# Taking the tensor work off GpSimd, and moving the adaLN gate from the output weights to the output

## The chip, the cores and the metric

One Trainium2 chip, one of its cores. The time of a kernel is the device time of one execution in microseconds (us), as the median of several runs. The engines are TensorE (PE, with its weight loads as PEld), VectorE (DVE), ScalarE (ACT), GpSimd (POOL) and SyncE (SP), which issues all DMAs here.

## The reference

One decoder layer on 256 tokens of width 1024, all in float32. The attention parts are left out here; there are two groups of 8 heads with 64 columns each, and group A has a mixture of dilated causal windows, group B plain causal attention (at 256 tokens there is only one block).

```python
mod = c @ w_ada + b_ada                          # (1, 3072)
shift, scale, gate = jnp.split(mod, 3, axis=-1)
h = x * (1.0 + scale) + shift
qa, ka, va, ga, qb, kb, vb, gb = jnp.split(h @ w_in, offs, axis=-1)   # 8 x 512 columns
qa, ka, qb, kb = _rope(qa), _rope(ka), _rope(qb), _rope(kb)
o_a = dilated_mixture(qa, ka, va) * silu(ga)
o_b = moba_attention(qb, kb, vb) * silu(gb)
y = jnp.concatenate([o_a, o_b], -1) @ w_out
x = layernorm(ALPHA * x + gate * y, ln_g, ln_b)
```

## The kernel before

**Precision.** A float32 matrix product is made of three products of a faster format (float32r). Each weight tile of 128 x 1024 (a buffer `raw`, 512 KB) is split: ACT copies it rounded to a buffer `whi`, and DVE or POOL subtracts that from the tile to get `wlo`, mostly in halves of 512 columns. `hH` and `hL` are the same two parts of h, `ogh` and `ogl` those of the gated attention output. PE multiplies `whi` with both parts of the other operand and `wlo` with its high part. `split_tile` is the function that splits; the lists `sp`, `wopool` in CFG say which subtractions POOL makes: 25 of 512 columns.

**Stages.** The first 60 us make h and its product with 1792 columns of w_in (q, k, v of group A and half of A's gate) in seven PSUM banks, `acc1`. Then come nine sets of 256 columns (list SETS), eight k-tiles each, and between their products PE gets the steps of eight attention pairs (two heads each): `att_pair` transposes the rotated q and k on PE (line 572 of before), `att_scores` multiplies them, DVE adds the mask and finds the maximum (`z`, line 598), ACT makes the exponentials (line 601), DVE a reciprocal (line 606), ACT scales; `att_trans` transposes the result (line 621), `att_pv` multiplies with v, DVE applies the silu gate (`og`) and the difference `ogl`. The rope is two DVE instructions: a product out of PSUM with a table (`pp`, line 514), which also frees the PSUM bank, and a sum of its halves (`rot`, line 256). `out_mm` multiplies with the eight row tiles of w_out, and `layer_norm(0)` and `layer_norm(1)` finish the token halves t=0 and t=1. Their parts are cut by CUTS: two of 512 columns for t=0; 512, 256, 256 for t=1.

**The gate.** `gate_acc(r)` adds c times one row tile of the last third of w_ada to a 128 x 1024 tile `gate`: ten halves by one DVE instruction each, six by a scaling on ACT and an addition on POOL. `gate_bcast` sums it over the partitions, by four products with a tile of ones (`onesr`), and `split_wo` multiplies each row tile of w_out by the result before it is split: seven halves and two whole tiles on DVE, five halves on POOL. ACT multiplies x by ALPHA (`scale_x`), and the layer norm adds that to y out of PSUM.

**What sets the order.** Nothing is decided at run time. The class `Plan` takes the operations in program order with a cost in ns for each (the first number given to `op`, `mm` or `tt`), works out due times from those of PE, and places one operation after another on its engine, with buffers from small pools: eight `raw`, six `whi`, six `wlo`, eight PSUM banks (`ps`), four `rot`. Each engine then executes its list in that order and waits by semaphores, so an instruction that waits holds up everything behind it on its engine. SP issues loads in the order of the `load_...` calls, each as soon as its `raw` buffer is free, and waits there otherwise. Lines 251 and 253 are copies on ACT, 256 two-operand operations on DVE or POOL (`tt`), 277 matmuls, 317 the loads.

Of the kernel before, what the change touches and what calls it, by code (L numbers as in the profile page):

```python
# [24 lines left out]
CFG = dict(raw=8, hdve=[3, 5, 6, 7], hl=6, a0=-6.0, ra=0.885, rb=1.15, s0=1, s1=5, gpos=1, wpool=[],  # L25
           sp=[[1, 2], [1, 2], [0, 1], [0, 1, 3], [1, 2], [0, 1], [1, 2], [0, 1, 3], [0, 1]],
           ropea=[0, 0, 0, 0], wopool=[[1], [0], [0], [1], [], [], [0], [1]], nf=2,
           jpe=[0, 1, 2, 0, 1, 1, 0, 2], pvo=[1, 0], pe0=1280, lock=1, wact=[], wsub=[], sact=[2, 6],
           ssub=[17], oact=[], osub=[0], gwhole=[1, 3], hamc=3300, lat=140, nst=4, nprob=2, nrot=4, nz=3,
           mact=[1, 2, 4, 5, 6], gdve=[1, 2, 3, 4, 6], nact=[0, 1, 2, 3], ropeb=[0, 1, 1, 1], norm='dve',  # L30
           t0=19000, late=0, lnp=1, warm=28, pt=2, wgpool=[[0], [0], [1], [0], [0], [], [0], [0]])
# [12 lines left out]
class Plan:  # L44
# [44 lines left out]
    def emit(self):  # L89
# [52 lines left out]
        def place(i):  # L142
# [37 lines left out]
            order.append((i, now, fin))  # L180

# [38 lines left out]
def hybrid_kernel(ctx: ExitStack, tc: tile.TileContext, x, c, w_in, w_out, w_ada, b_ada, ln_g, ln_b,  # L220
# [67 lines left out]
    onesr = consts.tile([128, 128], F32R)  # L288
# [81 lines left out]
    def modulate(k):  # L370
# [96 lines left out]
    def split_set(i, u):  # L467
# [3 lines left out]
                   2 * i + u in CFG["ssub"], [q for q in range(2) if 2 * u + q in CFG["sp"][i]])  # L471

    def split_wo(r):
        hi, lo = T["woh", r] = hi_lo()
        b = T["wo", r]
        for qs, cs in [((0, 1), slice(0, 1024))] if r in CFG["gwhole"] else [((q,), slice(q * 512, q * 512 + 512)) for q in range(2)]:
            e = POOL if len(qs) == 1 and qs[0] in CFG["wgpool"][r] else DVE
            tt(e, lambda cs=cs: b.ap[:, cs], lambda cs=cs: b.ap[:, cs], lambda cs=cs: gate[:, cs], OP.mult,
               vcost(e, cs.stop - cs.start), [("gate", q) for q in qs] + [(b, 0)], [(b, 0)])
        split_tile(hi, lo, b, lambda: b.ap, 1024, r in CFG["oact"], r in CFG["osub"], CFG["wopool"][r])  # L480

    def gate_acc(r):
        b = T["gate", r]
        for n in range(2):
            cs = slice(n * 512, (n + 1) * 512)
            if r in CFG["gdve"]:
                op(DVE, 663, lambda cs=cs: nc.vector.scalar_tensor_tensor(
                    gate[:, cs], b.ap[:, cs], cc[:, r:r + 1], gate[:, cs], op0=OP.mult, op1=OP.add),
                    [(b, n), "c", ("gate", n)], [("gate", n)], p2=True)
                continue  # L490
            copy(lambda cs=cs: b.ap[:, cs], lambda cs=cs: b.ap[:, cs], 613, [(b, n), "c"], [(b, n)],
                 scale=lambda: cc[:, r:r + 1])
            tt(POOL, lambda cs=cs: gate[:, cs], lambda cs=cs: gate[:, cs], lambda cs=cs: b.ap[:, cs], OP.add,
               1225, [(b, n), ("gate", n)], [("gate", n)])
# [14 lines left out]
    def rope_group(key, srcs, eng):  # L509
# [359 lines left out]
```

## Time and profile before

| what | value |
|---|---|
| median of 3 runs | 186.26 us (186.22 to 186.55) |
| profiled execution | 186.19 us |
| its span, first to last instruction | 184.3 us |
| mean granted TensorE clock | 0.951 |
| busy: PE / DVE / ACT / POOL | 164.2 / 144.2 / 107.5 / 67.2 us |

The span is what the views of the trace divide up; 1.89 us of the profiled execution lie around it. A busy time is the union of an engine's instructions. The granted clock is given as a share of TensorE's full speed: 1.00 is its upper level of 2.4 GHz, and about 0.5 its lower one of 1.2 GHz.

### The profile page before, as it was taken

What the parts mean: (1) busy time and instruction counts of PE and PEld (TensorE: products, weight loads), DVE (VectorE), ACT (ScalarE), POOL (GpSimd) and SP (SyncE); (2) the same over time, 40 slices, a digit from 0 to 9 for tenths busy, and PEclk for the clock granted to TensorE, in tenths of its full rate; (3) what the DMA queues carried; (4) which work ended last, traced back from release to release, by engine and by line L of the source; (5) the groups of instructions that cost most, each with busy time, mean ns of one, the idle gap of its engine ahead of it and who ended that gap; (6) DMA issues with size and microseconds to landing.
All of it is one profiled execution on the core that took longest, in us unless ns stands there. A gap on an engine that the chain in (4) does not pass through costs nothing.

```text
span 184.3 us, 3133 instructions
## 1 busy us (share of the span) xinstructions
PE 164.2 (89%) x1061; PEld 137.9 (75%) x1061; DVE 144.2 (78%) x305; ACT 107.5 (58%) x263; POOL 67.2 (36%) x55
## 2 busy tenths in 40 slices
PE   7758898899999999939999999999999859999950
PEld 2346786688888899927989689789988648778840
DVE  1449789899998699999489994569797983487883
ACT  3044744556666965715897689995489463990000
POOL 3000000000000897580033685970359980041460
PEclk9999999999999999975999999999999965999995
DMA  3999999999999999266457777670600600000022
GB/s 98 267 327 358 322 331 345 340 327 325 341 350 349 348 348 378 74 225 185 136 183 234 237 244 268 218 241 8 211 17 5 228 0 0 0 4 0 0 114 114
DMA packets 33429, 37.31 MB, mean 202 GB/s; under 512 B 1645, under 2 KB 28293, under 8 KB 33414
## 3 DMA queue, kind: packets, MB, share of 16 engines
q1 hardware_dynamic: 33414, 37.12, 63.3%
q8 instruction: 8, 0.13, 0.3%
q14 instruction: 7, 0.06, 0.1%
HBM read 36.07 MB, written 1.05 MB: 201 GB/s over the span
## 4 chain that ended last, share of the span: by engine, by line
PE 59%; DVE 14%; DMA 14%; SPq 5%; ACT 2%; POOL 2%; issue 2%; DVEq 0%; ACTq 0%
PE ps L277 54%; DMA raw<-in_w_in_dram 10%; DVE wlo L256 6%; SPq L317 5%; DMA raw<-in_w_ada_dram 4%; PE ps L621 3%; DVE rot L256 3%; POOL wlo L256 2%; PE ps L572 2%; DVE pp L514 1%; ACT whi L251 1%; DVE ogl L256 1%; DVE z L598 0%; DVE raw L693 0%; DVE raw L696 0%
## 5 line engine op out<-in xcount | busy, mean ns | idle before, releaser
L256 POOL TENSOR_TENSOR wlo<-raw,whi 128x512 fp32r<-128x512 f32 x25 | 37.9, 1542 | 86.4 <-DVE hL L256 58.3
L251 ACT ACTIVATE whi<-raw 128x512 fp32r<-128x512 f32 (+1 forms) x82 | 45.5, 612 | 17.0 <-DMA raw<-in_w_in_dram 12.0
L256 DVE TENSOR_TENSOR wlo<-raw,whi 128x512 fp32r<-128x512 f32 (+2 forms) x57 | 47.8, 866 | 8.0 <-ACT whi L251 7.8
L277 PE MATMUL ps<-whi,hH 128*128 128x256 f32 (+1 forms) x144 | 40.2, 335 | 2.1 <-ACT hH L251 1.9
L277 PE MATMUL ps<-wlo,hH 128*128 128x256 f32 (+1 forms) x144 | 41.9, 337 | 0.0
L277 PE MATMUL ps<-whi,hL 128*128 128x256 f32 (+1 forms) x144 | 40.0, 329 | 0.0
L277 PEld LDWEIGHTS ps<-whi,hH 128*128 128x128 f32 x144 | 26.6, 196 | 5.6 <-ACT hH L251 3.0
L277 PEld LDWEIGHTS ps<-whi,hL 128*128 128x128 f32 x144 | 26.6, 194 | 3.2 <-issue 1.4
L277 PEld LDWEIGHTS ps<-wlo,hH 128*128 128x128 f32 x144 | 26.7, 196 | 2.6 <-issue 1.4
L383 DVE SCALAR_TENSOR_TENSOR acc<-raw,cc,acc 128x256 f32<-128x256 f32 x49 | 23.6, 483 | 3.0 <-ACT acc L253 1.7
L601 ACT ACTIVATE prob<-z,st 128x256 f32<-128x256 f32 (+1 forms) x32 | 14.2, 447 | 11.8 <-DVE st L598 6.3
L277 PE MATMUL ps<-hL,whi 128*128 128x256 f32 x64 | 17.8, 300 | 0.0
L277 PE MATMUL ps<-hH,whi 128*128 128x256 f32 x64 | 17.5, 292 | 0.0
L277 PE MATMUL ps<-hH,wlo 128*128 128x256 f32 x64 | 17.0, 291 | 0.0
L253 ACT ACTIVATE prob<-prob,st 128x256 f32<-128x256 f32 (+1 forms) x32 | 12.1, 444 | 3.4 <-DVE st L606 3.3
L277 PE MATMUL ps<-whi,ogh 128*128 128x512 f32 (+1 forms) x40 | 12.9, 362 | 0.0
L277 PE MATMUL ps<-wlo,ogh 128*128 128x512 f32 (+1 forms) x40 | 12.8, 365 | 0.0
L277 PEld LDWEIGHTS ps<-hH,whi 128*128 128x128 f32 x64 | 11.7, 190 | 1.5 <-issue 1.2
L598 DVE CUSTOM_DVE_ANT_0 z<-ps,mask_t 128x256 f32<-128x256 f32 (+1 forms) x32 | 9.6, 348 | 3.7 <-PE ps L277 3.7
L277 PEld LDWEIGHTS ps<-hL,whi 128*128 128x128 f32 x64 | 11.6, 190 | 1.2 <-issue 1.0
L277 PE MATMUL ps<-whi,ogl 128*128 128x512 f32 (+1 forms) x40 | 12.4, 356 | 0.0
L277 PEld LDWEIGHTS ps<-hH,wlo 128*128 128x128 f32 x64 | 11.7, 191 | 0.3
(84 smaller groups left out, 263.6 us busy)
## 6 DMA issues: line engine op xcount, KB each, us to landing
raw<-in_w_in_dram SPq DMA_DIRECT2D x26, 512.0 KB, 7.4
raw<-in_w_ada_dram SPq DMA_DIRECT2D x32, 256.0 KB, 7.0
raw<-in_w_ada_dram SPq DMA_DIRECT2D x8, 512.0 KB, 5.6
raw<-in_w_out_dram SPq DMA_DIRECT2D x8, 512.0 KB, 3.8
raw<-in_w_in_dram SPq DMA_DIRECT2D x8, 384.0 KB, 5.9
out_dram<-raw SPq DMA_DIRECT2D x4, 256.0 KB, 2.1
xs<-in_x_dram SPq DMA_DIRECT2D x1, 512.0 KB, 7.0
raw<-in_ln_g_dram SPq DMA_DIRECT2D x1, 512.0 KB, 3.6
```

The source lines that it names most:

```text
L251: op(ACT, dur, lambda: nc.scalar.activation(o(), i(), AF.Copy), r, w)
L253: op(ACT, dur, lambda: nc.scalar.activation(o(), i(), AF.Copy, scale=scale()), r, w)
L256: op(e, dur, lambda: vec[e].tensor_tensor(o(), a(), b(), alu), r, w, p2=p2)
L277: f = lambda: nc.tensor.matmul(o(), a(), b(), start=start, stop=stop, skip_group_check=True)
L317: op(SP, kb * 1024 / 0.36e3, lambda: nc.sync.dma_start(o(), src), [], w)
L383: op(DVE, 396, lambda src=src, j=j: nc.vector.scalar_tensor_tensor(acc.ap[:, 0:2], src(), cc[:, j:j + 1], acc.ap[:, 0:2], op0=OP.mult, op1 ...
L514: op(DVE, 602, lambda b=b, c0=c0, pp=pp, t=t: nc.vector.tensor_tensor(pp.ap.rearrange("p c h a d -> p c h (a d)"), b.ap[:, c0:c0 + 256].re ...
L572: pe(109, lambda i=i, t=t, r=r: nc.tensor.transpose(b.ap[:, (2 * i + t) * 128:(2 * i + t + 1) * 128], r.ap.rearrange("p t h a d -> p t (h ...
L598: op(DVE, n / 0.96 + 76, lambda e=e, t=t, i=i, c=c: nc.vector.tensor_tensor_reduce(z[e].ap[:, c], b[e].ap[:, c], m[:, 128 - 128 * t:], -0. ...
L601: op(ACT, n * 0.833 + 280, lambda e=e, t=t, i=i, c=c: nc.scalar.activation(p[e].ap[:, c], z[e].ap[:, c], AF.Exp, bias=st.ap[:, i:i + 1], s ...
L621: pe(109, lambda i=i: nc.tensor.transpose(b.ap[:, i * 128:(i + 1) * 128], p.ap[:, i * 128:(i + 1) * 128], ident), [(p, 1 if i else 0)], [( ...
```

## The change

- POOL keeps only four tiny operations and two additions or products of 512 columns in the layer norm. The 25 `wlo` subtractions, six rope sums and six gate additions go to DVE; all 16 gate halves are one DVE instruction each now.
- w_out is no longer multiplied by the gate. `gate_bcast` is two plain float32 products of 512 columns instead of four float32r ones, without the splitting of the gate. It stands behind all of t=0's output products.
- The layer norm multiplies y by the gate out of PSUM, and one more DVE instruction (line 656 of after) adds ALPHA times x. ACT no longer scales x.
- Loads: all sets first, then the eight row tiles of w_out, then the eight gate tiles, then ln_g and ln_b. Before, gate tiles stood between the sets, and ln_g and ln_b ahead of the last two w_out tiles.
- Costs of PE operations in the plan are raised (216 to 232 for a 512-column product, 109 to 120 for 256, those of scores and pv by more), which moves the places of the other engines' work.

```diff
-           sp=[[1, 2], [1, 2], [0, 1], [0, 1, 3], [1, 2], [0, 1], [1, 2], [0, 1, 3], [0, 1]],
-           ropea=[0, 0, 0, 0], wopool=[[1], [0], [0], [1], [], [], [0], [1]], nf=2,
...
-            e = POOL if not sub and qs[0] in pool else DVE
-            tt(e, lambda cs=cs: lo.ap[:, cs], lambda cs=cs: src()[:, cs], lambda cs=cs: hi.ap[:, cs].bitcast(F32),
...
+            tt(DVE, lambda cs=cs: lo.ap[:, cs], lambda cs=cs: src()[:, cs], lambda cs=cs: hi.ap[:, cs].bitcast(F32),
...
-            tt(e, lambda cs=cs: b.ap[:, cs], lambda cs=cs: b.ap[:, cs], lambda cs=cs: gate[:, cs], OP.mult,
...
-            for u in range(2):
-                mm(216, [(hl, u), "onesr"], [(b, 0)], lambda b=b: b.ap, lambda: onesr, lambda hl=hl, u=u: hl.ap[:, u],
-                   u == 0, u == 1)
+            mm(900, [("gate", n)], [(b, 0)], lambda b=b: b.ap, lambda: ones, lambda cs=cs: gate[:, cs], True, True)
...
-            tt(DVE, lambda cs=cs: r.ap[:, cs], lambda b=b: b.ap, lambda cs=cs: xs[:, t, cs], OP.add, d,
-               [(b, 0), ("xa", t)], [(r, n)], False)
+            tt(DVE, lambda cs=cs: r.ap[:, cs], lambda b=b: b.ap, lambda cs=cs: gate[:, cs], OP.mult, d,
+               [(b, 0)] + [("gate", q) for q in range(2) if c0 < 512 * q + 512 and c1 > 512 * q], [(r, n)], False)
+            op(DVE, d + 60, lambda cs=cs: nc.vector.scalar_tensor_tensor(
+                r.ap[:, cs], xs[:, t, cs], ALPHA, r.ap[:, cs], op0=OP.mult, op1=OP.add),
+                [(r, n), ("x", 0), ("x", 1), ("x", 2)], [(r, n)], p2=True)
...
-    for i in range(5):
+    for i in range(9):
         load_set(i)
-    for i in range(4):
-        load_gate(2 * i)
-        load_gate(2 * i + 1)
-        load_set(i + 5)
-    for r in range(6):
+    for r in range(8):
         load_wo(r)
+    for r in range(8):
+        load_gate(r)
     load_ln(0)
     load_ln(1)
-    load_wo(6)
-    load_wo(7)
...
     for i in (6, 7):
         out_mm(i, 0)
+    for r in range(8):
+        gate_acc(r)
+    gate_bcast()
     layer_norm(0)
```

The order of instructions moves on DVE at three places that the prediction speaks of. The first is DVE at the end of the first product, where the sets' first splits (`wlo`) and the rope of A (`pp`, `rot`) begin; a number behind a name tells buffers apart, and x2 is two halves. Before:

```order
L256 TENSOR_TENSOR wlo_685<-raw_573,whi_674 128x512
L256 TENSOR_TENSOR hL<-acc_604,hH 128x256
L256 TENSOR_TENSOR wlo_707<-raw_592,whi_696 128x512
L514 TENSOR_TENSOR pp_718<-ps_211,rope_t 128x512
L514 TENSOR_TENSOR pp_724<-ps_221,rope_t 128x512
L256 TENSOR_TENSOR wlo_730<-raw_607,whi_713 128x512
L256 TENSOR_TENSOR wlo_754<-raw_636,whi_727 128x512
L256 TENSOR_TENSOR rot_766<-pp_718 128x256
L256 TENSOR_TENSOR rot_766<-pp_724 128x256
L514 TENSOR_TENSOR pp_777<-ps_216,rope_t 128x512
L514 TENSOR_TENSOR pp_787<-ps_225,rope_t 128x512
L532 SCALAR_TENSOR_TENSOR sga_95<-sga_95,ps_230 128x256 x2
```

After:

```order
L254 TENSOR_TENSOR wlo_684<-raw_571,whi_677 128x512 x2
L254 TENSOR_TENSOR wlo_696<-raw_593,whi_688 128x512 x2
L496 TENSOR_TENSOR pp_713<-ps_209,rope_t 128x512
L254 TENSOR_TENSOR wlo_721<-raw_600,whi_705 128x512 x2
L254 TENSOR_TENSOR wlo_733<-raw_620,whi_719 128x512 x2
L496 TENSOR_TENSOR pp_753<-ps_221,rope_t 128x512
L254 TENSOR_TENSOR rot_765<-pp_713 128x256
L254 TENSOR_TENSOR rot_765<-pp_753 128x256
L496 TENSOR_TENSOR pp_774<-ps_214,rope_t 128x512
L496 TENSOR_TENSOR pp_781<-ps_223,rope_t 128x512
L254 TENSOR_TENSOR rot_788<-pp_774 128x256
L254 TENSOR_TENSOR rot_788<-pp_781 128x256
```

DVE now has eight halves of `wlo` where it had four, ahead of the first two rope sums, and the first silu step (`sga`) has gone further back.

The second place is DVE ahead of the mask and maximum (`z`) of the last attention pair but one. Before (`raw_1324`, `raw_1359`, `raw_1405`, `raw_1432` and `raw_1503` are tiles of w_out):

```order
L256 TENSOR_TENSOR raw_1503<-raw_1503,gate 128x512
L514 TENSOR_TENSOR pp_1703<-ps_1491,rope_t 128x512
L256 TENSOR_TENSOR og_1730<-ps_1719,sgb_97 128x256
L256 TENSOR_TENSOR wlo_1744<-raw_1324,whi_1691 128x1024
L256 TENSOR_TENSOR wlo_1762<-raw_1359,whi_1656 128x512
L256 TENSOR_TENSOR wlo_1773<-raw_1405,whi_1736 128x512
L256 TENSOR_TENSOR wlo_1781<-raw_1432,whi_1725 128x512
L256 TENSOR_TENSOR ogl<-og_1663,ogh 128x256
L598 ISA z_1794,st_1795<-ps_1783,mask_t 128x256
```

After, ahead of the `z` of the same pair (`raw_1193`, `raw_1267` are tiles of w_out, `raw_1529`, `raw_1561`, `raw_1624` the first gate tiles):

```order
L478 SCALAR_TENSOR_TENSOR gate<-raw_1529,cc,gate 128x512 x2
L496 TENSOR_TENSOR pp_1651<-ps_1468,rope_t 128x512
L496 TENSOR_TENSOR pp_1663<-ps_1468,rope_t 128x512
L254 TENSOR_TENSOR rot_1671<-pp_1651 128x256
L254 TENSOR_TENSOR rot_1671<-pp_1663 128x256
L254 TENSOR_TENSOR wlo_1682<-raw_1267,whi_1649 128x512 x2
L254 TENSOR_TENSOR ogl<-og_1622,ogh 128x256
L478 SCALAR_TENSOR_TENSOR gate<-raw_1561,cc,gate 128x512
L254 TENSOR_TENSOR og_1713<-ps_1675,sgb_96 128x256
L478 SCALAR_TENSOR_TENSOR gate<-raw_1624,cc,gate 128x512
L478 SCALAR_TENSOR_TENSOR gate<-raw_1561,cc,gate 128x512
L580 ISA z_1724,st_1725<-ps_1707,mask_t 128x256
```

Four splits and an `ogl` in one block have become two halves of a split, an `ogl` and gate halves; the other gate halves follow behind, the last of them ahead of the splits of the last three tiles of w_out.

The third place is the end of DVE's list, the layer norm of t=1 (its last two rows, for ln_g and ln_b, are left out). Before:

```order
L256 TENSOR_TENSOR raw_2031<-ps_1713,xs 128x512
L256 TENSOR_TENSOR raw_2031<-ps_1734,xs 128x256
L677 BN_STATS bn_2044<-raw_2031 128x6 x2
L256 TENSOR_TENSOR raw_2031<-ps_1739,xs 128x256
L677 BN_STATS bn_2044<-raw_2031 128x6
L679 BN_AGGR mv_2062<-bn_2044 128x2
```

After (`gate` is the summed gate, `xs` is x):

```order
L254 TENSOR_TENSOR raw_2005<-ps_1828,gate 128x512
L254 TENSOR_TENSOR raw_2005<-ps_1854,gate 128x256
L656 SCALAR_TENSOR_TENSOR raw_2005<-xs,raw_2005 128x512
L656 SCALAR_TENSOR_TENSOR raw_2005<-xs,raw_2005 128x256
L254 TENSOR_TENSOR raw_2005<-ps_1862,gate 128x256
L659 BN_STATS bn_2029<-raw_2005 128x6 x2
L656 SCALAR_TENSOR_TENSOR raw_2005<-xs,raw_2005 128x256
L659 BN_STATS bn_2029<-raw_2005 128x6
L661 BN_AGGR mv_2036<-bn_2029 128x2
```

The statistics (BN_STATS) of the first two parts stood ahead of the last part's step out of PSUM, and now stand behind it, and each part has one more instruction.

## Rows read from the trace of the kernel before

**Rows 1.** The page, parts 1 and 2: busy time of the engines; granted TensorE clock in 40 slices.

```profile
PE 164.2 (89%) x1061; PEld 137.9 (75%) x1061; DVE 144.2 (78%) x305; ACT 107.5 (58%) x263; POOL 67.2 (36%) x55
...
PEclk9999999999999999975999999999999965999995
```

**Rows 2.** Stretches (us): length, busy PE, PEld, DVE, ACT, POOL, PEclk, DMA share, GB/s.

```profile
82.00:88.00 6.00, 5.98 (x28) 5.07 (x29) 6.00 (x23) 2.76 (x10) 0.32 (x1) 0.51 0.66 219
88.00:146.40 58.40, 58.20 (x471) 51.65 (x471) 45.94 (x100) 47.07 (x128) 33.85 (x24) 1.00 0.52 171
...
149.60:156.20 6.60, 6.60 (x26) 5.38 (x27) 3.01 (x15) 3.35 (x13) 1.87 (x2) 0.51 0.00 0
156.20:177.50 21.30, 21.25 (x127) 17.35 (x125) 15.12 (x26) 8.82 (x25) 6.88 (x6) 1.00 0.00 1
```

**Rows 3.** Timeline of PE: start, length, instruction, idle time before it and releaser.

```profile
81.94 1.09 PE L572 MATMUL ps<-ident,rot 128*128 128x128 f32 x4 [3.03 <-DVE pp L514]
...
149.58 0.79 PE L277 MATMUL ps<-qk 64*128 64x128 f32 x3 [2.74 <-DVE st L598]
```

**Rows 4.** Chain of work that ended last: start, length, what.

```profile
71.71 2.04 DVE rot L256 x2
...
78.39 2.81 DVE rot L256 x2
81.20 0.61 DVE pp L514
...
140.73 6.50 DVE wlo L256 x4
147.23 1.40 DVE ogl L256
```

**Rows 5.** Groups of DVE instructions, 13 to 60 us: count, busy, mean ns.

```profile
L256 DVE TENSOR_TENSOR wlo<-raw,whi 128x512 fp32r<-128x512 f32 x25 | 16.3, 686 | 3.3 <-ACT whi L251 3.1
```

**Rows 6.** Groups of DVE instructions, 62.9 to 85.4 us.

```profile
L256 DVE TENSOR_TENSOR rot<-pp 128x256 f32<-128x256 f32 x8 | 8.7, 1125 | 0.0
L256 DVE TENSOR_TENSOR wlo<-raw,whi 128x512 fp32r<-128x512 f32 x6 | 7.7, 1310 | 0.0
L514 DVE TENSOR_TENSOR pp<-ps,rope_t 128x512 f32<-128x512 f32 x10 | 6.4, 678 | 0.6 <-PE ps L277 0.6
```

**Rows 7.** Groups of DVE instructions, 93.5 to 150 us.

```profile
L487 DVE SCALAR_TENSOR_TENSOR gate<-raw,cc,gate 128x512 f32<-128x512 f32 x10 | 10.0, 1048 | 0.0
```

**Rows 8.** Timeline of DVE at 82.3 us.

```profile
82.32 0.74 DVE L256 TENSOR_TENSOR rot<-pp 128x256 f32<-128x256 f32 x2
```

**Rows 9.** Groups of DVE instructions, whole span.

```profile
L256 DVE TENSOR_TENSOR wlo<-raw,whi 128x512 fp32r<-128x512 f32 x47 | 42.0, 922 | 8.0 <-ACT whi L251 7.8
```

**Rows 10.** Timeline of POOL, at its first tensor work and near the end.

```profile
60.48 9.10 POOL L256 TENSOR_TENSOR wlo<-raw,whi 128x512 fp32r<-128x512 f32 x6 [58.27 <-DVE hL L256]
...
163.37 1.49 POOL L256 TENSOR_TENSOR wlo<-raw,whi 128x512 fp32r<-128x512 f32 x1 [11.90 <-ACT whi L251]
...
174.02 3.11 POOL L256 TENSOR_TENSOR raw<-raw,raw 128x512 f32<-128x512 f32 x2 [0.66 <-DVE raw L685]
```

**Rows 11.** Timeline of PE: two float32r products of 512 columns, and plain float32 ones.

```profile
157.93 0.62 PE L277 MATMUL ps<-wlo,ogh 128*128 128x512 f32 x2
...
159.66 0.87 PE L277 MATMUL ps<-pt,vvb 128*64 128x128 f32 x8
```

**Rows 12.** Timeline of DVE near the end.

```profile
163.63 1.50 DVE L256 TENSOR_TENSOR ogl<-og,ogh 128x256 fp32r<-128x256 f32 x1
...
176.04 1.01 DVE L677 BATCH_NORM_STATS2 bn<-raw 128x6 f32<-128x512 f32 x2
177.49 0.42 DVE L256 TENSOR_TENSOR raw<-ps,xs 128x256 f32<-128x256 f32 x1 [0.45 <-PE ps L277]
```

**Rows 13.** The page, part 6: loads, KB each, us from issue to landing.

```profile
raw<-in_w_ada_dram SPq DMA_DIRECT2D x8, 512.0 KB, 5.6
raw<-in_w_out_dram SPq DMA_DIRECT2D x8, 512.0 KB, 3.8
```

More of the change, by code (lines that the diff above doesn't have):

```diff
@@ L180, in place @@
             order.append((i, now, fin))
+            self.order = order
         wake = []
@@ L426, in split_w @@
             b = T["w", k, i]
-            split_tile(hi, lo, b, lambda b=b: b.ap, n, 2 * k + i in CFG["wact"], 2 * k + i in CFG["wsub"],
-                       [q for q in range(2) if 2 * i + q in CFG["wpool"]])
+            split_tile(hi, lo, b, lambda b=b: b.ap, n, False, False)
     def proj1(k):
@@ L470, in split_set @@
         split_tile(hi, lo, b, lambda: b.ap.rearrange("p k n -> p (k n)"), 1024, 2 * i + u in CFG["sact"],
-                   2 * i + u in CFG["ssub"], [q for q in range(2) if 2 * u + q in CFG["sp"][i]])
+                   2 * i + u in CFG["ssub"])
     def split_wo(r):
@@ L475, in split_wo @@
         b = T["wo", r]
-        for qs, cs in [((0, 1), slice(0, 1024))] if r in CFG["gwhole"] else [((q,), slice(q * 512, q * 512 + 512)) for q in range(2)]:
-            e = POOL if len(qs) == 1 and qs[0] in CFG["wgpool"][r] else DVE
-            tt(e, lambda cs=cs: b.ap[:, cs], lambda cs=cs: b.ap[:, cs], lambda cs=cs: gate[:, cs], OP.mult,
-               vcost(e, cs.stop - cs.start), [("gate", q) for q in qs] + [(b, 0)], [(b, 0)])
-        split_tile(hi, lo, b, lambda: b.ap, 1024, r in CFG["oact"], r in CFG["osub"], CFG["wopool"][r])
+        split_tile(hi, lo, b, lambda: b.ap, 1024, False, False)
     def gate_acc(r):
@@ L485, in gate_acc @@
             cs = slice(n * 512, (n + 1) * 512)
[L486 to L494, printed above, removed]
+            op(DVE, 663, lambda cs=cs: nc.vector.scalar_tensor_tensor(
+                gate[:, cs], b.ap[:, cs], cc[:, r:r + 1], gate[:, cs], op0=OP.mult, op1=OP.add),
+                [(b, n), "c", ("gate", n)], [("gate", n)], p2=True)
     def gate_bcast():
@@ L518, in rope_group @@
                 [(b, 0), "rope"], [(pp, 0)])
[L519 to L520 removed]
+            tt(DVE, lambda t=t: r.ap[:, t], lambda pp=pp: pp.ap[:, 0], lambda pp=pp: pp.ap[:, 1][:, :, ::-1],
+               OP.add, 335, [(pp, 0)], [(r, t)])
     def keep_v(y, t, g, n, b, c0):
@@ L559, in set_finish @@
         else:
-            rope_group((nm, g), [(b, 0), (b, 256)], POOL if CFG["ropeb"][("qkab".index(nm[0])) + 2 * g] else DVE)
+            rope_group((nm, g), [(b, 0), (b, 256)])
     qk, ptt, ogp, prob = {}, {}, {}, {}
@@ L752, in finish_a @@
     def finish_a(g):
-        rope_group(("qa", g), [(acc1[t], g * 256) for t in range(2)], POOL if CFG["ropea"][2 * g] else DVE)
-        rope_group(("ka", g), [(acc1[2 + t], g * 256) for t in range(2)], POOL if CFG["ropea"][2 * g + 1] else DVE)
+        rope_group(("qa", g), [(acc1[t], g * 256) for t in range(2)])
+        rope_group(("ka", g), [(acc1[2 + t], g * 256) for t in range(2)])
     for t in range(2):
@@ L771, in hybrid_kernel @@
     at(8, 4, split_wo, 1)
-    for r in range(8):
-        at(CFG["gpos"] + r // 2, 2 + 4 * (r % 2), gate_acc, r)
-    at(CFG["gpos"] + 4, 7, gate_bcast)
     def idle():
@@ L822, in hybrid_kernel @@
     att_next(100)
-    for t in range(2):
-        scale_x(t)
     for i in (6, 7):
         out_mm(i, 0)
+    for r in range(8):
+        gate_acc(r)
+    gate_bcast()
     layer_norm(0)
```

45 lines of the change are left out of this document (18 added, 27 removed).

## The prediction

> **What bounds the kernel now.** I read the page first. PE is busy for 164.2 of 184.3 us, DVE for 144.2, POOL for 67.2, and the strip of granted clock shows two dips, in the slices 18 and 19 and again in 33 to 35 of 40 [rows 1]. So this is a kernel bound by PE, with two accidents. The view by stretches sizes them: between them, from 88.0 to 146.4 us, PE is busy for 58.20 of 58.4 us at clock 1.00, and from 156.2 to the last product at 177.5 for 21.25 of 21.3. But 82.0 to 88.0 and 149.6 to 156.2 run at 0.51, the lower level [rows 2]. What came ahead of each is in PE's timeline: one idle time of 3.03 us that ends at 81.94, one of 2.74 us that ends at 149.58, both released by DVE [rows 3]. In each case PE had worked without a break at the upper level, stood still, and was granted the lower level from its restart on, for 6.0 and 6.6 us.
>
> The chain of work says why DVE was late. Ahead of the first stall it does, from 71.71 on, two rope sums in 2.04 us and, after splits and rope products, two more in 2.81, and only then the rope product (0.61) that frees the PSUM bank which the transposes of line 572 want. Ahead of the second it does four splits in 6.50 us and an `ogl` in 1.40, with the `z` steps queued behind them [rows 4]. These prices are the point. While POOL has no tensor work, a DVE split of 512 columns is 16.3 / 25 = 0.65 us [rows 5]. Between 62.9 and 85.4, with POOL at work, it is 7.7 / 6 = 1.28, and a rope sum 8.7 / 8 = 1.09, but the rope product, which reads PSUM, stays at 6.4 / 10 = 0.64 [rows 6]. The gate instruction costs 1.0 from 93.5 to 150 [rows 7]. When POOL rests, two rope sums take 0.74 together [rows 8]. So DVE instructions with two inputs in SBUF about double beside POOL, and those with one don't.
>
> **The change part by part.** *DVE's load.* The 22 half splits after 60 us cost 42.0 − 16.3 = 25.7 us [rows 5, 9]; at 0.65 they are 14.3, so 11.4 come back. Ten gate halves give back about 3.3 (1.0 to an estimated 0.67, by the split's price) and the ten rope sums about 6 (1.0 to 0.37). New on DVE are 25 splits (16.3), six rope sums (2.2), six gate halves (4.0) and five additions of x in the layer norm (three of 512 and two of 256 columns, about 3.0); gone are the multiplications of w_out (seven halves, two whole tiles) and two halves of the gate's split, 8.5 at the price of 0.65 a half. The balance is 25.5 − 8.5 − 20.7 = −3.7: DVE stays below its present 144 [rows 1], though POOL's 67 us all but vanish. ACT only loses work.
>
> *First stall, −3.0.* POOL's first split starts at 60.48 [rows 10], so a DVE split can start then too. By the order of the change, up to the rope product that frees the bank, DVE has 12 half splits (7.8), seven rope products (4.5) and six rope sums (2.2): 14.5, which ends at about 75.0, where before it ended at 81.81. PE comes to this place at 78.9 before. The bank is free 3 to 4 us ahead, and the last rope sums, about 0.7 later, are also in time. If the cover fails (a later `whi` copy), each us late is a us on PE.
>
> *Second stall, −2.7.* The order puts two half splits (1.3), an `ogl`, an `og` (0.4 each) and three gate halves (2.0) ahead of this `z`, about 4.1 against 7.9 before, and some of it ahead of the scores' arrival. I reckon the `z` steps to be at most 1.4 us behind their scores, less than the products that PE has meanwhile.
>
> *The clock, −6.2.* If PE does not stand still, the 6.0 us at 0.51 shrink by 2.9 and the 6.6 by 3.2 [rows 2].
>
> *The gate sum, +1.0.* Four products of 512 columns at 0.23 us each (two in a row take 0.62, one of them 0.39 from first to last [rows 11]) go; two in plain float32 come. No plain float32 product of this shape is in the trace. The nearest row is eight records of a pair's pv products, 0.87 us for 128 and 256 columns of two heads side by side [rows 11]; 512 / 384 of that is 1.16 each. The lower bound is the float32r price, 0.23 each. I take 0.95 each, near the row: 1.9 − 0.9 = 1.0, between −0.5 and +1.4.
>
> *The gate's loads, 0.* The gate tiles are last but for ln_g and ln_b, and each waits for a `raw` buffer: the first four for those of the w_out tiles, the others for those of earlier gate tiles. A tile of w_out landed 3.8 us after issue, a gate tile, beside other loads, 5.6 [rows 13]. By 3.8 I get all sums done at about 147 us, with PE's products of the gate at about 154: 7 us of cover. The splits of the last three w_out tiles stand behind the sums on DVE; PE wants the first of them at about 150.2, 2.4 us after I have it. So the move is hidden at 3.8, and not far above it (see below).
>
> *Small waits, +0.7.* The plan has become just in time: I find the first pair's `z` with some 0.2 us to spare, and later steps within 0.5. PE had 0.2 us of idle time in 58.4 [rows 2]; I allow 0.7, between 0 and 2.
>
> *The end, +2.8.* Behind PE's last product DVE had one addition out of PSUM (0.42) and one set of statistics before the mean; the other two (1.01 together) lay ahead of it [rows 12]. They now stand behind the last part's product, +1.0, and that part has one more instruction, +0.4. The two additions of x for the first two parts (about 1.2) fill DVE's present pause of 0.45 and add 0.75. That makes +2.1. Then POOL: its two operations for t=0 take 3.11 us [rows 10], and DVE's neighbours at that place before read PSUM, and were not slowed. The new additions read two SBUF inputs. What that can cost is seen where a POOL split from 163.37 to 164.86 lay beside an `ogl` that began at 163.63 and took 1.50 [rows 10, 12], against 0.42 for its size: it ended after POOL did. Two additions of DVE stand there and POOL has two operations of 1.55 each; laid against each other by the times above, DVE's waits come to 1.9 at most. I take 0.7, as I place DVE's additions late in POOL's work: +2.8, between +2.1 and +4.0.
>
> The Trainium skill (SBUF — State Buffer, "Who interferes with whom") speaks against this end: it says that a VectorE instruction with two SBUF inputs and a GpSimd instruction that reads SBUF share an exclusive lock, so that whichever starts second is blocked for the whole of the other. By that rule the full 1.9 is paid, +4.0, and the total would be 1.2 us higher. The row with the 1.50 agrees with it; the rope product beside POOL, with one SBUF input, agrees with its other half.
>
> *Sum.* 184.3 − 5.8 − 6.2 + 1.0 + 0.7 + 2.8 = 176.8 us of span, and with the 1.89 around it 178.7. The profiled execution (186.19) and the median (186.26) differ by nothing here.
>
> **The rivals.** *A, better still (under 175.5).* The plain products cost as little as the old ones and DVE's pause swallows most of the end: −0.5 and +0.4 in place of +1.0 and +2.8, no small waits, 174.1. Against it: the pv row, and the order of the statistics. *B, one stall stays or comes up elsewhere.* PE's idle time of 2 us or more, and then some 3 us of lower clock, as both stalls show: 183.7 to 184.7. The places are the first `z` steps, where I have least to spare, and the splits behind the gate sums. For it speaks that DVE now carries all subtractions, in list order. *C, no change.* POOL's help is worth what its interference cost, and DVE's additional 25 us bring back both stalls elsewhere: about 186. Against it: the balance above, by which DVE has less to do than before. *D, slower.* The gate tiles land late. Three of them follow one another through one buffer, so a landing time that is L longer moves the last sum by about 3 L, and all behind it on DVE, the splits that PE wants among them, with 2.4 to 2.8 us of cover. Slower than 186.6 needs a stall of 5 us and 3 of lower clock: L of 2.6 us, a landing of 6.4. For it speaks the 5.6 of gate tiles before; against it, that those shared the queues with the sets' loads, and these have none beside them but the last w_out tiles.
>
> **How the numbers follow.** The forecast (both stalls gone) has a chance of 0.66, and by its own bounds 175.5 to 181.5. A has 0.05, B 0.14, C 0.05, D 0.10. Predicted is 178.7; the range of 175.5 to 184.7 holds the forecast and B. Faster by over 0.2%, which is about what a measurement of this kernel can tell from no change: the forecast, A and B, 0.85; within it C, 0.05; slower D, 0.10.
>
> **What would show it.** Right: granted clock of 1.00 from 36 us to the last product, no idle time of PE above 1 us there, a DVE split of 0.65 throughout, a rope sum of 0.37, and about 9.6 us from the last product to the end, where 6.8 stood. The gate sums end near 147 us, and two pairs of records of about 0.95 us precede the products of t=1. Wrong: a dip of the clock anywhere, which means a stall that I have not seen; a PE wait for `wlo` behind gate sums (D); or a loaded tile that lands in 6 us or more near 130.

## The result, and the profile after

The changed kernel takes 178.65 us (177.86 to 179.86, four runs), the kernel before 186.41 (186.22 to 186.83) beside it: a ratio of 0.959, with an interval of 0.952 to 0.965. The profiled execution has 179.19 us and a span of 177.4. Predicted were 178.7 and a span of 176.8. Ratios, here and below, leave out executions that took over 1.5% longer than the fastest one of their kernel measured along with them, so they can differ from the ratio of the medians.

The page of the changed kernel, parts 1 and 2 (busy time, and the granted clock in 40 slices):

```profile
PE 160.9 (91%) x1061; PEld 135.3 (76%) x1061; DVE 137.8 (78%) x337; ACT 100.4 (57%) x252; POOL 7.2 (4%) x13
...
PEclk9999999956999999999999999999999999999995
```

Against [rows 1], POOL's 67.2 us are 7.2, and DVE, which took them over, has *less* busy time than before. Both late dips of the clock are gone, but there is a new one, early. The view by stretches (us, busy PE, PEld, DVE, ACT, POOL, granted clock, DMA share, GB/s):

```profile
36.00:42.90 6.90, 6.71 (x20) 5.53 (x20) 4.94 (x11) 2.99 (x7) 0.00 (x0) 0.51 1.08 332
42.90:79.00 36.10, 36.10 (x232) 32.74 (x233) 33.29 (x73) 20.02 (x39) 0.00 (x0) 1.00 1.02 319
79.00:157.70 78.70, 78.70 (x611) 68.37 (x610) 61.15 (x174) 60.35 (x173) 0.00 (x0) 1.00 0.46 148
```

From 42.9 to 157.7 us PE is busy without any gap, at clock 1.00; [rows 2] had 0.51 for 6.0 and 6.6 us in that range, and [rows 3] two idle times. The price of DVE's instructions over the whole span (count, busy, mean ns):

```profile
L254 DVE TENSOR_TENSOR wlo<-raw,whi 128x512 fp32r<-128x512 f32 x74 | 47.9, 687 | 9.9 <-ACT whi L249 9.6
L478 DVE SCALAR_TENSOR_TENSOR gate<-raw,cc,gate 128x512 f32<-128x512 f32 x16 | 11.3, 747 | 0.0
L496 DVE TENSOR_TENSOR pp<-ps,rope_t 128x512 f32<-128x512 f32 x16 | 10.4, 682 | 1.3 <-PE ps L275 1.3
L254 DVE TENSOR_TENSOR rot<-pp 128x256 f32<-128x256 f32 x16 | 6.0, 418 | 0.0
```

A split is 47.9 / 74 = 0.65 us over the whole span, where it was 1.28 beside POOL [rows 6]; a rope sum 0.37 instead of 1.09, a gate half 0.71 instead of 1.0 [rows 7]. The rope product out of PSUM is 0.65, as it was.

The new dip is at 36.0 to 42.9. PE's timeline ahead of it (start, length, instruction, idle time and releaser):

```profile
35.65 0.44 PE L362 MATMUL ps<-ident,xs 128*128 128x128 f32 x2 [1.24 <-DVE md L254]
```

In the kernel before, the same step starts at 35.71 after 0.65 us:

```profile
35.71 0.44 PE L365 MATMUL ps<-ident,xs 128*128 128x128 f32 x2 [0.65 <-DVE md L256]
```

Both wait for the same small DVE result (`md`), which hangs on a load of w_ada that lands at about the same time (34.4 us) in both; PE only gets there earlier now. What this costs by the end of the first stage is read from DVE's timelines, at the last part of h (`hL` of the eighth k-tile), in the changed kernel, in the one before, and in a kernel with the changed order of work whose trace has no dip there (POOL's writes, below):

```profile
61.94 0.43 DVE L254 TENSOR_TENSOR hL<-acc,hH 128x256 fp32r<-128x256 f32 x1 [0.28 <-ACT hH L392]
```

```profile
60.02 0.42 DVE L256 TENSOR_TENSOR hL<-acc,hH 128x256 fp32r<-128x256 f32 x1
```

```profile
59.71 0.42 DVE L254 TENSOR_TENSOR hL<-acc,hH 128x256 fp32r<-128x256 f32 x1
```

Without the dip the changed order is not later than the kernel before; with it, it is 1.9 us later.

So the account has three parts. Up to the last part of h: +1.9 us. From there to the end of PE's last product (before: 60.02 to 177.45; after: 61.94 to 168.24): 117.4 to 106.3, −11.1. Behind it: 6.85 to 9.16, +2.3. That is the 6.9 by which the span is shorter.

The end, in the timelines of DVE and then of POOL:

```profile
159.42 0.69 DVE L254 TENSOR_TENSOR raw<-ps,gate 128x512 f32<-128x512 f32 x1 [4.09 <-ACT gate L251]
...
166.23 1.01 DVE L254 TENSOR_TENSOR raw<-ps,gate 128x512 f32<-128x512 f32 x2
167.16 2.25 DVE L656 SCALAR_TENSOR_TENSOR raw<-xs,raw 128x512 f32<-128x512 f32 x2
169.34 0.41 DVE L254 TENSOR_TENSOR raw<-ps,gate 128x256 f32<-128x256 f32 x1
169.68 1.00 DVE L659 BATCH_NORM_STATS2 bn<-raw 128x6 f32<-128x512 f32 x2
170.60 0.40 DVE L656 SCALAR_TENSOR_TENSOR raw<-xs,raw 128x256 f32<-128x256 f32 x1
171.03 0.43 DVE L659 BATCH_NORM_STATS2 bn<-raw 128x6 f32<-128x256 f32 x1
```

```profile
165.87 3.27 POOL L254 TENSOR_TENSOR raw<-raw,raw 128x512 f32<-128x512 f32 x2 [0.80 <-DVE raw L667]
```

Behind the last product, at 168.24, stand the rest of two additions of x that took 2.25 us beside POOL, the last part's product, two sets of statistics and the last part's own two steps. DVE works from 159.42 on with one short wait for POOL (0.72): it is the limit of this stage.

### The profile page after: what moved, and what is told of

Same layout as the page of the kernel before. It is cut to its first block, busy times and chain, and to the rows that moved or that the text cites. A ratio compares the mean times of both kernels' runs of the same rounds, so it can differ in the third digit from the quotient of the medians.

```text
span 177.4 us, 3091 instructions
## 1 busy us (share of the span) xinstructions
PE 160.9 (91%) x1061; PEld 135.3 (76%) x1061; DVE 137.8 (78%) x337; ACT 100.4 (57%) x252; POOL 7.2 (4%) x13
## 3 DMA queue, kind: packets, MB, share of 16 engines
HBM read 36.07 MB, written 1.05 MB: 209 GB/s over the span
## 4 chain that ended last, share of the span: by engine, by line
PE 69%; DMA 12%; DVE 7%; SPq 5%; ACT 2%; issue 1%; POOL 1%; DVEq 0%; ACTq 0%; POOLq 0%
PE ps L275 64%; DMA raw<-in_w_in_dram 8%; SPq L314 5%; DMA raw<-in_w_ada_dram 4%; PE ps L603 3%; DVE raw L656 2%; PE ps L554 2%; DVE bn L659 2%; DVE raw L254 1%; ACT whi L249 1%; DVE raw L678 1%; POOL mv L254 1%; DVE raw L675 0%; DVEq L840 0%; ACT hH L392 0%
## 5 line engine op out<-in xcount | busy, mean ns | idle before, releaser
L254 DVE TENSOR_TENSOR wlo<-raw,whi 128x512 fp32r<-128x512 f32 (+1 forms) x83 | 52.2, 667 | 10.4 <-ACT whi L249 10.1
L275 PE MATMUL ps<-whi,hH 128*128 128x256 f32 (+1 forms) x144 | 41.5, 339 | 1.6 <-ACT hH L249 1.4
L275 PE MATMUL ps<-whi,hL 128*128 128x256 f32 (+1 forms) x144 | 42.1, 335 | 0.0
L275 PEld LDWEIGHTS ps<-whi,hL 128*128 128x128 f32 x144 | 27.1, 196 | 2.6 <-issue 0.7
L275 PE MATMUL ps<-whi,ogl 128*128 128x512 f32 (+1 forms) x40 | 13.2, 362 | 0.0
L496 DVE TENSOR_TENSOR pp<-ps,rope_t 128x512 f32<-128x512 f32 x16 | 10.4, 682 | 1.3 <-PE ps L275 1.3
L478 DVE SCALAR_TENSOR_TENSOR gate<-raw,cc,gate 128x512 f32<-128x512 f32 x16 | 11.3, 747 | 0.0
```

Of the source, the lines that this page charges most:

```text
L254: op(e, dur, lambda: vec[e].tensor_tensor(o(), a(), b(), alu), r, w, p2=p2)
L275: f = lambda: nc.tensor.matmul(o(), a(), b(), start=start, stop=stop, skip_group_check=True)
L478: op(DVE, 663, lambda cs=cs: nc.vector.scalar_tensor_tensor(gate[:, cs], b.ap[:, cs], cc[:, r:r + 1], gate[:, cs], op0=OP.mult, op1=OP.add ...
L496: op(DVE, 602, lambda b=b, c0=c0, pp=pp, t=t: nc.vector.tensor_tensor(pp.ap.rearrange("p c h a d -> p c h (a d)"), b.ap[:, c0:c0 + 256].re ...
```

## The experiments

**POOL busy with reads of its own.** Every engine's list stays as it is in the changed kernel; POOL gets 40 additions.

```diff
+    s0, s1 = (consts.tile([128, 512], F32, name=f"scr{n}", tag=f"scr{n}") for n in range(2))
...
+            tt(POOL, lambda: s1, lambda: s0, lambda: s0, OP.add, 1225, [key], ["scr"], False)
...
+    busy_pool(16, ("hL", 7))
...
+    for i in (0, 2, 4):
+        busy_pool(8, ("ogh", i))
```

> The changed kernel with every engine's list as it was, and 40 additions of 128x512 more on POOL, from 60 us on, on two tiles that nobody else uses (its output is that of the reference). Theory 1, DVE was slowed by POOL's reading of SBUF: a DVE split of 512 columns rises from 0.65 to 1.1 to 1.3 us wherever POOL is busy, the rope products out of PSUM stay at 0.64; with some 60 us of POOL work DVE needs about 20 us more, so PE gets stalls of several us and dips of the clock behind them: 185 to 196 us. Theory 2, the gain came from the moved gate and the new order of work, and POOL's activity does not matter: 178 to 180 us, a split stays at 0.65.

Measured: 199.15 us (198.81 to 199.36), 1.073 times the kernel before (1.066 to 1.081). The two tiles hang on nothing, so POOL began at once and was busy in the first 51 us, not from 60 on. The groups of that stretch, and POOL's:

```profile
L380 DVE SCALAR_TENSOR_TENSOR acc<-raw,cc,acc 128x256 f32<-128x256 f32 x20 | 23.2, 1161 | 0.6
L254 DVE TENSOR_TENSOR wlo<-raw,whi 128x512 fp32r<-128x512 f32 x9 | 13.2, 1507 | 0.0
...
L254 POOL TENSOR_TENSOR scr<-scr 128x512 f32<-128x512 f32 x40 | 46.3, 1158 | 3.1
```

A split is 13.2 / 9 = 1.47 us there, an addition of the modulation 1.16 against 0.48 in the changed kernel, and PE waited 11.3 us in all for the sums of the modulation. The place was another than I meant and the time lies above the 185 to 196 expected; the slowing of DVE is the one expected.

**POOL busy with writes only.**

```diff
-            tt(POOL, lambda: s1, lambda: s0, lambda: s0, OP.add, 1225, [key], ["scr"], False)
+            op(POOL, 1225, lambda: [nc.gpsimd.memset(s1, 0.0) for _ in range(3)][-1], [key], ["scr"])
```

> The same with POOL only writing: 40 times three memsets of 128x512 on an unused tile in place of the additions, so POOL is as busy but reads nothing. Theory 1 in its narrow form (only a POOL instruction that reads SBUF is in DVE's way): 178 to 180 us, a split stays at 0.65. A wider form (any busy POOL slows DVE): slowed as with the additions, 185 us or more.

Measured: 177.14 us (176.84 to 177.94), 0.956 of the kernel before (0.949 to 0.963), a little less than the 178 to 180 expected. The groups of DVE from 8 to 75 us, when POOL was at work, and of POOL:

```profile
L254 DVE TENSOR_TENSOR wlo<-raw,whi 128x512 fp32r<-128x512 f32 x36 | 23.2, 685 | 2.5 <-ACT whi L249 2.4
...
L732 POOL MEMSET s<- 128x512 f32 x120 | 63.3, 528 | 6.8
```

POOL was busy for 63.3 us and cost DVE nothing: a split is 23.2 / 36 = 0.64. So it is not POOL's being busy that slows DVE, but its reading of SBUF (all of POOL's reading instructions here have two inputs in SBUF; one input was not tried). The Trainium skill (SBUF — State Buffer, "Who interferes with whom") says that VectorE with two SBUF inputs contends with a GpSimd instruction that reads SBUF, not with one that only writes it; these two runs agree with both halves.

**The reads again, where they were meant.** The operands are now tiles that exist only at that time.

```diff
+            tt(POOL, lambda: scr.rearrange("p (a b) -> p a b", a=2), lambda: src().bitcast(F32),
+               lambda: src().bitcast(F32), OP.add, 1225, [key], ["scr"], False)
...
+    busy_pool(16, lambda: hL[:, 6:8], ("hL", 7))
...
+    for i in (1, 3, 5):
+        busy_pool(8, lambda i=i: ogl[:, i - 1:i + 1], ("ogl", i))
```

> The changed kernel with every engine's list as it was, and 40 additions of 128x512 more on POOL that read SBUF: 16 that can start when the last part of h is there, near 61 us, and three times 8 behind the second, fourth and sixth attention pair (its output is that of the reference). Theory 1: beside them a DVE split takes 1.1 to 1.3 us instead of 0.65, and the rope products 0.64 as before; the first z steps come 5 us or more late, PE stalls near 80 us with a dip of the clock behind it: 184 to 195 us. Theory 2 (DVE's slowness beside POOL has no part in the gain): within 1 us of the changed kernel.

Measured: 194.98 us (193.38 to 195.40), 1.049 (1.041 to 1.058). DVE's groups from 60 to 85 us, with POOL busy from 61.6 to 82.9, and from 85 to 110, with POOL at rest, in the same execution:

```profile
L254 DVE TENSOR_TENSOR wlo<-raw,whi 128x512 fp32r<-128x512 f32 x12 | 16.2, 1408 | 0.1
L254 DVE TENSOR_TENSOR rot<-pp 128x256 f32<-128x256 f32 x4 | 4.2, 1087 | 0.0
L496 DVE TENSOR_TENSOR pp<-ps,rope_t 128x512 f32<-128x512 f32 x6 | 3.9, 677 | 0.0
...
L254 DVE TENSOR_TENSOR wlo<-raw,whi 128x512 fp32r<-128x512 f32 x14 | 8.8, 682 | 0.1
L254 DVE TENSOR_TENSOR rot<-pp 128x256 f32<-128x256 f32 x8 | 3.0, 413 | 0.0
L496 DVE TENSOR_TENSOR pp<-ps,rope_t 128x512 f32<-128x512 f32 x7 | 4.6, 675 | 0.0
```

A split is 1.35 and then 0.63, a rope sum 1.05 and then 0.38, and the product out of PSUM 0.65 in both. PE's waits of that kernel (line waited for, us in total, times, longest):

```profile
PE ps L275 <- DVE pp L496: 5.2, 1, 5.2
...
PE ps L275 <- DVE st L580: 1.8, 1, 1.8
```

They are waits for the same two steps as in [rows 3], a rope product and a `z`, now both at the first pairs, and the clock is at 0.50 for 6.8 us from 82.0 on. The order of work was that of the changed kernel, so that order alone does not keep the stalls away; POOL's reads bring them back.

**The kernel before, with POOL's work on DVE.** The gate still multiplies w_out.

```diff
-           sp=[[1, 2], [1, 2], [0, 1], [0, 1, 3], [1, 2], [0, 1], [1, 2], [0, 1, 3], [0, 1]],
-           ropea=[0, 0, 0, 0], wopool=[[1], [0], [0], [1], [], [], [0], [1]], nf=2,
+           sp=[[]] * 9,
+           ropea=[0, 0, 0, 0], wopool=[[]] * 8, nf=2,
...
-           mact=[1, 2, 4, 5, 6], gdve=[1, 2, 3, 4, 6], nact=[0, 1, 2, 3], ropeb=[0, 1, 1, 1], norm='dve',
-           t0=19000, late=0, lnp=1, warm=28, pt=2, wgpool=[[0], [0], [1], [0], [0], [], [0], [0]])
+           mact=[1, 2, 4, 5, 6], gdve=[1, 2, 3, 4, 6], nact=[0, 1, 2, 3], ropeb=[0, 0, 0, 0], norm='dve',
+           t0=19000, late=0, lnp=1, warm=28, pt=2, wgpool=[[]] * 8)
```

> The kernel before, with its POOL splits, rope sums and multiplications of w_out given to DVE (lists sp, wopool, ropeb and wgpool empty); the gate still multiplies w_out and is loaded between the sets, and POOL keeps six gate additions and the layer norm. The plan orders the work anew. Theory 1: both stalls and both dips of the clock go, unless the heavier DVE list makes one of its own: 174 to 178 us, or about 180 to 181 with one dip left. Theory 2 (the gate's move is what helped): 185 to 187.

Measured: 177.13 us (176.60 to 177.88), 0.955 of the kernel before (0.948 to 0.962). Its granted clock in 40 slices:

```profile
PEclk9996999999999999999999999999999999999985
```

One part of the change alone gives all of its gain, though POOL keeps its six gate additions here (10.6 us). The moved gate, the layer norm's new steps and the new costs add nothing that these runs can tell.

**POOL's work back in the changed kernel.** The splits and rope sums of before return to POOL; gate, loads and costs stay.

```diff
-            tt(DVE, lambda cs=cs: lo.ap[:, cs], lambda cs=cs: src()[:, cs], lambda cs=cs: hi.ap[:, cs].bitcast(F32),
...
+            e = POOL if not sub and qs[0] in pool else DVE
+            tt(e, lambda cs=cs: lo.ap[:, cs], lambda cs=cs: src()[:, cs], lambda cs=cs: hi.ap[:, cs].bitcast(F32),
...
-            rope_group((nm, g), [(b, 0), (b, 256)])
+            rope_group((nm, g), [(b, 0), (b, 256)], POOL if ROPEB["qkab".index(nm[0]) + 2 * g] else DVE)
```

> The changed kernel with 25 splits and six rope sums back on POOL, as before; gate, loads and plan costs stay as changed (the plan orders the work anew). Theory 1: DVE beside POOL at about twice its price again, at least one stall of 2 us with its dip: 181 to 188 us. Theory 2: 177 to 180.

Measured: 183.91 us (182.84 to 185.26, ten runs); against the kernel before 1.001 (0.994 to 1.009). DVE's groups from 60 to 150 us, and then PE's waits:

```profile
L257 DVE TENSOR_TENSOR wlo<-raw,whi 128x512 fp32r<-128x512 f32 x18 | 17.9, 1014 | 5.6 <-ACT whi L252 5.5
...
L257 DVE TENSOR_TENSOR rot<-pp 128x256 f32<-128x256 f32 x10 | 9.4, 967 | 0.0
```

```profile
PE ps L278 <- DVE pp L500: 1.9, 1, 1.9
PE ps L558 <- DVE pp L500: 1.6, 1, 1.6
```

A split costs 17.9 / 18 = 0.99 and a rope sum 0.94 over that stretch, in which POOL is at work for part of the time. Two stalls are back, of 1.9 and 1.6 us, and from the last part of h PE needs 112.0 us instead of 106.3. I had expected one of 2 us or more with its dip: no dip of the clock followed these in the profiled execution, so a stall does not always bring one. Most of the gain is gone again: the kernel with POOL's writes, measured along with it, took 177.14.

**The changed kernel again,** twice, as a base.

> The changed kernel once more, as a base on this chip. The dip of the clock at 36 us, which follows an idle time of PE of 1.24 us, is either a fixed part of this kernel (then it is in this trace as well, and the mean clock of every run is near 0.967), or hangs on chance (then the mean clocks differ from run to run, with the time: 0.985 to 0.99 near 175 to 176 us, 0.967 near 178 to 179).

> The changed kernel again, as the base for the kernels of this call: 177 to 180 us, with a dip of the clock near 36 us in most executions.

Measured: 178.75 us (176.92 to 180.29) with a ratio of 0.955 (0.947 to 0.964), and 178.58 (178.33 to 181.07) with 0.972 (0.965 to 0.978). The traces have a dip of 6.8 us at 36.8 and one of 3.4 at 37.5; the first kernel with the same lists (POOL's writes) had none, after an idle time of 1.08 us there. Of all nine traces in which PE idles there for at least 1.0 us, seven have a dip; of the four in which it idles for 0.65 or less and POOL does not read in that stage, none has. What decides in one execution, these traces do not show. Nor does the dip account for the spread of the times: the mean clocks are 0.970 to 0.973 in the executions near 177 us and 0.966 to 0.967 in those near 180, not the 0.985 against 0.967 that I expected. What does not vary is the rest: from the last part of h to PE's last product it is 106.3 us in all three traces of the changed kernel.

**PE kept busy at 34.4 us.**

```diff
+        if k == 2:
+            for _ in range(6):
+                op(PE, 1, lambda: nc.tensor.matmul(acc1[0].ap, warm[:, 0:128], warm, start=False, stop=False,
+                                                   skip_group_check=True), [], [(acc1[0], 0)], cols=0)
```

> The changed kernel with six products of zeros (bf16, 128x512, added to a PSUM bank in use, output unchanged) where PE stood idle for 1.24 us at 34.4 us. If that idle time brings the dip of the clock at 36 us, the dip goes and the runs are alike: a mean clock of 0.985 or more, 175.5 to 176.5 us. If the dip has another cause, or the products only delay PE: a dip as before, 177.9 to 179.9 us.

Measured: 177.58 us (177.10 to 177.88), 0.957 (0.952 to 0.962). The clock in 40 slices:

```profile
PEclk9987999999999999999999999999999999999975
```

The dip at 36 us is gone, and none of the four executions takes 180 us; but this trace has another dip of 3.4 us at 11.6, behind PE's wait of 3.6 us for x. The time is not as low as I wrote. That the dip at 36 comes behind the idle time agrees with this trace, and with that of the two repairs below, in both of which the idle time and the dip are gone together; two traces alone would not show it, since POOL's writes had the one without the other.

**The layer norm's POOL operations on DVE.**

```diff
-           mact=[1, 2, 4, 5, 6], nact=[0, 1, 2, 3], t0=19000, late=0, lnp=1, warm=28, pt=2)
+           mact=[1, 2, 4, 5, 6], nact=[0, 1, 2, 3], t0=19000, late=0, lnp=0, warm=28, pt=2)
```

> The changed kernel with lnp=0: POOL's last two tensor operations (those of the layer norm of t=0) are made by DVE. Theory 1, POOL's reads are in the way of the new additions of x: these two take 1.05 us together instead of 2.17, DVE has 0.9 us more to do, no wait for POOL's tiny operations: the end after PE's last product shrinks from 9.2 to 8.2 to 8.7 us. Rival, DVE is the only limit there: the end grows to about 10.

Measured: 176.83 us (175.49 to 177.62), 0.952 (0.944 to 0.961). DVE's additions of x for the first two parts:

```profile
166.18 1.02 DVE L656 SCALAR_TENSOR_TENSOR raw<-xs,raw 128x512 f32<-128x512 f32 x2
```

1.02 us instead of 2.25, though DVE has more to do. PE's last product ends at 167.32 and the span at 175.8: an end of 8.5 us instead of 9.2, as theory 1 has it.

**The plan's old PE costs.**

```diff
-            mm(232, [(hh, k), (w, q)], [(acc1[2 * n + t], 0)], lambda: acc1[2 * n + t].ap,
+            mm(216, [(hh, k), (w, q)], [(acc1[2 * n + t], 0)], lambda: acc1[2 * n + t].ap,
```

(and the six other costs likewise)

> The changed kernel with the PE costs of the plan as they were before (216, 109, 215 and 110, 107 and 215, /2.37, 214). If the raised costs only fit the order to the chip: some small waits of PE, 0 to 3 us slower than the changed kernel, no stall of 2 us. If the order of work was what took the stalls away: at least one stall of 2 us or more with its dip, 182 us or more.

Measured: 176.43 us (175.73 to 177.41), 0.959 (0.949 to 0.968), beside 0.972 (0.965 to 0.978) for the changed kernel measured along with it. PE has no stall of 2 us, as expected for costs that only shape the order; but I had expected 0 to 3 us more, and got about 2 less. In its trace PE needs 106.9 us from the last part of h, a little more, and the end is 8.3 instead of 9.2. The raised costs bring nothing here.

**Gate tiles that come late.**

```diff
-        load(lambda: b.ap, ada_v[:, r, 2 * DM:], 512, [(b, 0), (b, 1)])
+        def twice():
+            nc.sync.dma_start(b.ap, ada_v[:, r, 2 * DM:])
+            return nc.sync.dma_start(b.ap, ada_v[:, r, 2 * DM:])
+        op(SP, 512 * 1024 / 0.36e3, twice, [], [(b, 0), (b, 1)])
```

> The changed kernel with each gate tile loaded twice into its buffer, so that it is there about 2.5 to 3.3 us later; the other engines' lists are as they were (output unchanged). My rival D: the last gate sum is 7 to 10 us later (three loads in a row through one buffer), the splits of w_out behind it are late for PE, a stall of 4 to 8 us with a dip of the clock: 183 to 190 us. If the loads have more cover than I reckoned: within 1 us of the changed kernel.

Measured: 194.06 us (193.75 to 195.76), 1.058 (1.047 to 1.068). PE's waits, and DVE's last gate sums:

```profile
PE ps L606 <- ACT prob L251: 8.4, 3, 5.5
PE ps L275 <- DVE wlo L254: 3.0, 1, 3.0
```

```profile
164.49 1.42 DVE L481 SCALAR_TENSOR_TENSOR gate<-raw,cc,gate 128x512 f32<-128x512 f32 x2 [2.65 <-DMA raw<-in_w_ada_dram]
```

The last sum ends at 165.9 instead of 149.7, and PE waits for a split behind the sums, but longest, 5.5 us, for a softmax result whose `z` steps and reciprocal stand behind gate sums on DVE. The time lies above the 183 to 190 expected, as the delay is 16 us and not 7 to 10: SP waits in order as well, and the second load of each tile stands behind the first, so the last seven tiles came one after another through its queue, some 5 us apart.

**Two repairs together:** the products of zeros and lnp=0.

> Two repairs together: the six products of zeros at 34.4 us and the layer norm's two POOL operations on DVE. If the two effects are independent, the end shrinks by 0.7 us and the slow executions with a dip at 36 us go: 175.5 to 177 us, with little spread, 1 to 2.5 us below the changed kernel.

Measured: 176.25 us (176.14 to 177.09), 0.960 (0.955 to 0.965), against 178.58 (178.33 to 181.07) for the changed kernel measured along with it. It beats the changed kernel by about 1.3%, and its slowest execution is faster than the other's fastest. The old costs alone, measured along with both, gave as much (176.43), so it is not shown that the effects of the two repairs add up.

## Why the prediction was right, step by step

**The time** was met, 178.65 against 178.7, and so was the direction. Errors of both signs stand behind the agreement, so that it is as close as 0.05 us is luck.

**Stalls and clock, −5.8 and −6.2, and small waits, +0.7:** the first two are right, since both idle times and the dips behind them are gone, and POOL's reads alone bring stalls and a dip back. The 6.2 holds for an execution with both dips, though. One of the 27 later executions of the kernel before took 182.2 us at a mean clock of 0.983; by that clock, an estimate, about 6 us of it were at the lower level, against 18 of the profiled execution's span by its 0.951. All four executions that the prediction was measured against lie within 0.6 us of each other; beside the faster later ones the gain is smaller. The clock also fell at 81.0 and 149.3, while PE still stood idle, and not from its restart on, as the prediction reads it; it changes no price, as PE had nothing to do then. The bank that PE's transposes want is free at 77.15 (by the end of its rope product), and PE takes it at 78.46: 1.3 us of cover, not 3 to 4, as the first stage ended 1.9 later. The last rope sums, which the same transposes need, end at 77.82. For small waits I allowed 0.7; PE has no idle time at all there.

**The gate sum, +1.0:** right in size. PE's timeline:

```profile
157.73 1.02 PE L275 MATMUL ps<-gate,ones 128*128 128x512 f32 x2
...
158.83 1.02 PE L275 MATMUL ps<-gate,ones 128*128 128x512 f32 x2
...
160.03 0.51 PE L275 MATMUL ps<-wlo,ogh 128*128 128x512 f32 x2
```

From 157.73 to 160.03 lie the two products and three others, two of 512 columns (0.23 each) and one of 256 (0.12): (2.30 − 0.58) / 2 = 0.86 each, so +0.8 against four of 0.23.

With the measured 0.8 and no small waits the middle stage comes to −5.8 − 6.2 + 0.8 = −11.2; the trace has −11.1, where I had −10.3.

**The end, +2.8:** it is +2.3. The statistics stand where the order put them, and the wait for POOL is real: the two additions took 2.25 instead of 1.02, 1.2 of the 1.9 that it could cost. One by one, on POOL and DVE:

```profile
165.87 1.59 POOL L254 TENSOR_TENSOR raw<-raw,raw 128x512 f32<-128x512 f32 x1 [0.80 <-DVE raw L667]
167.16 0.85 DVE L656 SCALAR_TENSOR_TENSOR raw<-xs,raw 128x512 f32<-128x512 f32 x1
167.54 1.59 POOL L254 TENSOR_TENSOR raw<-raw,raw 128x512 f32<-128x512 f32 x1
167.94 1.48 DVE L656 SCALAR_TENSOR_TENSOR raw<-xs,raw 128x256 f32<-128x256 f32 x1
```

The first addition began 0.3 us before POOL's first operation ended and took 0.85, where such an addition with POOL at rest takes 0.67; the second, of 256 columns, began 0.4 us into POOL's second, took 1.48 instead of 0.40 and ended 0.3 us after it. That agrees with the exclusive lock of the Trainium skill (SBUF — State Buffer, "Who interferes with whom"). The 1.9 was the most that it could cost, and the additions were not placed for that; the prediction's "by that rule the full 1.9 is paid" does not follow. Part of the 2.25 also lies ahead of PE's last product: behind it, the rest of the two additions is 1.1 (I had 0.75 and 0.7 for POOL), and the statistics and the one more instruction are 1.2 instead of 1.4.

**What failed is a term that the sum does not have:** the first stage was taken as unchanged. PE gets to the step at 34.4 us earlier, idles longer for the same loads, and the clock falls for 6.9 us; the stage ends 1.9 later than before, and 2.2 later than in the trace of POOL's writes, which has no dip. That outweighs the 0.8 that the middle and the 0.5 that the end came out better, by 0.6: 177.4 against 176.8 of span. "A dip of the clock anywhere, which means a stall that I have not seen" was on my list of signs against me, and this is one.

**The rivals.** B (one stall left) describes this early dip, at a place that I did not name and at a third of its price. C is refuted, as DVE's busy time went from 144.2 to 137.8. That is −6.4 where the balance said −3.7: it left out the `ogl` steps (5.4 us before, 3.3 after) and put the multiplications of w_out at their price at rest, 8.5 where they took 9.8. D is a real mechanism: late tiles cost 15 us in the run that loaded each twice. It did not come up because the tiles land early:

```profile
raw<-in_w_ada_dram SPq DMA_DIRECT2D x8, 512.0 KB, 3.3
```

3.3 us, where they took 5.6 beside the sets' loads [rows 13]. The last sum ends at 149.7, 2.7 later than the 147 I had, and the gate's product starts at 157.7. PE waited for none of the splits behind the sums.

## What to carry to other kernels

Work given to a second engine was not free here, as its reads stood in the way of the first engine's: price the first engine's instructions with the helper at rest and at work, by their operands, before counting the relief. Where PE is the bound, an idle time is worth more than its length if the granted clock falls behind it, and a new order of work can shift PE into an idle time that is paced by loads. A total that agrees is no proof of its terms; compare the stages one by one.

## What the runs showed of the hardware

POOL's memsets, 63 us of them, slowed no DVE split (0.64 us), while its additions took it to 1.35 and 1.47. Products out of PSUM stayed at 0.65. The changed order showed dips of the clock at one place of 0, 3.4 or 6.8 us after idle times of 1.06 to 1.28 us, with mean clocks from 0.958 to 0.988 over its executions; the kernel before ranged from 182.2 to 189.0 us in the later measurements, with clocks from 0.984 to 0.933.
